# A sixth place for layer 1's split weight units, and one query buffer fewer

## The chip, the core and the metric

The kernel runs on one core of one Trainium2 chip. The metric is device time in microseconds (us) of one execution, and a kernel stands by the median of its runs. All texts below call the engines as the profile does: PE is TensorE (PEld its weight loads), DVE is VectorE, ACT is ScalarE, POOL is GpSimd, SP is SyncE, which here issues the DMAs.

## What is computed

The reference is a two-layer transformer block over 512 latent tokens and 256 context tokens of width 1024, in float32. Layer 0 is a mixer of windowed and dense grouped-query attention, layer 1 is differential attention over 8 heads, and a SwiGLU feed-forward follows each of them. The change lies in layer 1's attention. Cut to that, the reference is:

```python
def _odd_mixer(hx, hc, w_in, w_out, qn, kn, ...):
    q, k, v = jnp.split(h @ w_in, [qs, 2 * qs], axis=-1)   # w_in: 1024 x 3072
    q = _rope(_rms(q.reshape(b, n, 8, 2, 64), qn), cos, sin)
    k = _rope(_rms(k.reshape(b, n, 8, 2, 64), kn), cos, sin)
    # per head: two softmaxes a = 0, 1 over context and latent keys
    s = jnp.einsum('bqhad,bkhad->bhaqk', qb, k) * scale
    p = jax.nn.softmax(s, axis=-1)
    a = p[:, :, 0] - lam * p[:, :, 1]
    o = jnp.einsum('bhqk,bkhe->bqhe', a, v)                # then RMS norm, @ w_out
```

Only the latent tokens have queries in layer 1, so a latent tile of 128 tokens is projected to 384 columns of a head (q, k, v) and a context tile to 256 (k, v).

## The kernel before

**Split products.** Each large product is done as three matmuls on values split into a high and a low part: the high part is a copy of the value in the matmul's float type, made on ACT, and the low part is value minus high part, made by a subtraction on DVE or POOL. `project` (line 460) does `hi*hi`, `hi*lo` and `lo*hi` for each of the 8 slices of 128 input features, 24 matmuls for a tile of 128 tokens.

**Weight units.** The weights of one head are four units, each of 256 input features by 384 columns. `weight1` (line 649) asks `unit` (line 361) for one: three DMAs of 128 KB into a raw tile (line 365; the raw tiles are a ring of two, shared with other loads), a copy on ACT into the high part `wih` (line 370) and a subtraction on POOL into the low part `wil` (line 371). The raw tile is free when the subtraction has read it. The high and the low parts stand in pools of their own, `whi` and `wlo`, each a ring of `WBUF` = 5 places. A unit can be split when a place is free, that is when the last matmul of an earlier unit has read it. The units of heads 0 to 7 are numbered 0 to 31 below, unit u of head h being 4h + u; the four of head 0 are split earlier, during the feed-forward of layer 0.

**Order of the work.** PE's order is written out by hand (`manual_schedule`). Head 0 is projected first, unit by unit for its latent tiles. From then on the projection of head h + 1 is threaded through the attention of earlier tiles in half tiles: `halves` (line 1579) gives 12 steps for a head, one for the first four feature slices of a token tile (units 0 and 1, 12 matmuls) and one for the other four (units 2 and 3). Three steps go with each of the 32 pairs of head and query tile (`scores`, `transposed`, `values`). All tiles of a head use all four units, so units 0 and 1 are read for the last time in the head's last step but one, and units 2 and 3 in its last step.

After a tile's second half, `Proj1.finish` (line 672) copies the sums out of PSUM (`qkv`, line 677, ACT), does the norm and the rotation (ACT, DVE, POOL), and splits the query into `qd` (a copy on ACT at line 685 and a subtraction on DVE at line 686) and the key into `kd` (line 688 on ACT, line 689 on POOL). PE transposes both into `qpt` and `kpt` (lines 696 and 702) at least five steps after the tile's own, in `turned`. `qd` has three buffers.

The order on ACT, DVE, POOL and SP is not written by hand: a planner lays each engine's queue out ahead of time, by program order as priority and by its own estimates of when operands and places are ready. An engine then works its queue strictly in that order, so one that arrives at an instruction early stands still.

**Pools.** Pools are stretches of SBUF, stacked from two sides. `mix1` (`at`, line 1569) holds the attention's `qt`, `e`, `PT` and `o1`; `mw1` (`wp`, line 1564) holds `qkv`, `qz`, `qy`, `qd` and `kd`. A later pool that lies over an earlier one waits tile by tile for what was there.

Of the kernel before, what the change touches and what calls it, by code (L numbers as in the profile page):

```python
# [12 lines left out]
F32R = mybir.dt.float32r  # L13
# [6 lines left out]
P = 128  # L20
# [7 lines left out]
HD = 64  # L28
# [23 lines left out]
def bc(ap, pos, n):  # L52

    dims = [list(d) for d in ap.ap]
    return AP(ap.tensor, ap.offset, dims[:pos] + [[0, n]] + dims[pos:])
# [8 lines left out]
def backbone(es: ExitStack, tc: tile.TileContext, x, c, ctx, c_ctx, mod_w, mod_b, norm_mix_w, norm_ffn_w,  # L64
# [3 lines left out]
    nc = tc.nc  # L68
# [24 lines left out]
    def acc_tile(name, n=512, one=None):  # L93

        if one is None:
            one = turn["acc"] = 1 - turn["acc"]
        return p_1.tile([P, 512], F32, name=name, tag=f"acc{one}")[:, :n]
# [4 lines left out]
    def tr_tile(name, shape, dt=F32, one=None):  # L102
        if one is None:
            one = turn["tr"] = 1 - turn["tr"]
        return p_1.tile(shape, dt, name=name, tag=f"tr{one}")

    @contextmanager
    def behind(*names):

        with ExitStack() as st:  # L110
            for name in names:
                if name in turn:
                    st.enter_context(tc.issue_after(turn[name].ins))
            yield

    def f32(ap):
        return ap.bitcast(F32)
# [243 lines left out]
    def unit(pool, views, shape, bufs, name, sub=None, new_tile=raw_tile):  # L361

        raw = new_tile(shape, name + "r")
        for dst, src in views(raw):
            turn["load"] = nc.sync.dma_start(dst, src)
        p_hi, p_lo = pool if isinstance(pool, tuple) else (pool, pool)
        hi = p_hi.tile(shape, F32R, name=name + "h", tag="whi", bufs=bufs)
        lo = p_lo.tile(shape, F32R, name=name + "l", tag="wlo", bufs=bufs)
        with behind("pool_scale"):
            nc.scalar.copy(hi, raw)  # L370
            (sub or nc.vector).tensor_sub(lo, raw, f32(hi))
        return hi, lo
# [44 lines left out]
    def rotate_all(raw, h0, n, t, wc, tb, pool):  # L417

        sq = pool.tile([P, n * HD], F32, name="sq", tag="qz", bufs=2)
        nc.scalar.activation(sq, raw, AF.Square)  # L420
        ss = small.tile([P, n], F32, name="qss", tag="qss")
        nc.vector.tensor_reduce(ss, sq.rearrange("p (h d) -> p h d", d=HD), AX.X, ALU.add)
        r = rsqrt(ss, n, 1.0 / HD, "q")
        y = pool.tile([P, n, HD], F32, name="qy", tag="qy", bufs=2)
        rh = raw.rearrange("p (h d) -> p h d", d=HD)
        if t >= NTX:
            nc.vector.tensor_tensor(y, rh, wc[:, h0:h0 + n], ALU.mult)
            return y, r
        z = pool.tile([P, n, HD], F32, name="qz", tag="qz", bufs=2)
        nc.vector.tensor_tensor(z.rearrange("p h (a b) -> p (h a) b", b=2),  # L430
                                swap_pairs(raw), tb[:, t, 1].rearrange("p h (a b) -> p (h a) b", b=2), ALU.mult)
        nc.vector.tensor_tensor(y, rh, tb[:, t, 0], ALU.mult)
        nc.vector.tensor_add(y, y, z)
        return y, r
# [214 lines left out]
    def weight1(h, u, wh, sub, new_tile=raw_tile):  # L649

        def views(raw):
            for j in range(3):
                yield raw[:, :, j * P:(j + 1) * P], od_w_in[
                    0, u * 256:(u + 1) * 256, j * D + h * P:j * D + (h + 1) * P].rearrange("(j p) n -> p j n", p=P)
        return unit(wh, views, [P, 2, 384], WBUF, "wi", sub, new_tile)

    class Proj1:
# [14 lines left out]
        def finish(self, t, ps):  # L672

            n, wp, kT, qs = self.width(t), self.wp.pool, self.kT, self.qs
            m, h0 = (n - P) // HD, 0 if t < NTX else 2
            raw = wp.tile([P, 384], F32, name="qkv", tag="qkv", bufs=4)
            nc.scalar.copy(raw[:, :n], ps[:, :n])  # L677
            nc.gpsimd.tensor_copy(self.vv[:, t, :], raw[:, n - P:n])
            y, r = rotate_all(raw[:, :n - P], h0, m, t, self.wc, self.tb, wp)
            nc.gpsimd.tensor_tensor(y, y, bc(r, 2, HD), ALU.mult)  # L680
            nq = m - 2
            if nq:
                qd = wp.tile([P, 2, 2, 2, HD], F32R, name="qd", tag="qd", bufs=3)
                yb = bc(y[:, 0:2], 2, 2)
                nc.scalar.copy(qd[:, 0], yb)
                nc.vector.tensor_sub(qd[:, 1], yb, f32(qd[:, 0]))
            kd = wp.tile([P, 2, 2, HD], F32R, name="kd", tag="kd", bufs=3)
            nc.scalar.copy(kd[:, :, 0, :], y[:, nq:nq + 2])
            nc.gpsimd.tensor_sub(kd[:, :, 1, :], y[:, nq:nq + 2], f32(kd[:, :, 0, :]))

            def transposes():
                if nq:
                    pt = tr_tile("qpt", [P, 2, 2, P], F32R)
                    for j in range(2):
                        for a in range(2):
                            nc.tensor.transpose(pt[:, j, a, :], qd[:, j, a].rearrange("p a d -> p (a d)"), identr)
                    qt = self.qp.tile([P, 2, 2, P], F32R, name="qt", tag="qt", bufs=5)
                    nc.scalar.copy(qt, f32(pt))
                    qs[t] = qt
                pk = tr_tile("kpt", [P, 2, P], F32R)  # L700
                for a in range(2):
                    nc.tensor.transpose(pk[:, a, :], kd[:, a].rearrange("p a d -> p (a d)"), identr)
                nc.scalar.copy(kT[:, :, t * P:(t + 1) * P], f32(pk))
            return transposes
# [344 lines left out]
    def way_out1(xs, hidr, pool, places_w, places_h):  # L1049
# [7 lines left out]
        def ready_hid(f):  # L1057
            def views(raw):
                yield raw, ffn_w_out[1, f * P:(f + 1) * P, :]
            if f < len(places_w):  # L1060
                raw = raw_tile([P, D], "wdr")
                turn["load"] = nc.sync.dma_start(raw, ffn_w_out[1, f * P:(f + 1) * P, :])
                w, h = places_w[f], places_h[f]
                split_into(w, raw.rearrange("p (k c) -> p k c", k=4))
                split_into(h, hidr[f].rearrange("p (k c) -> p k c", k=2))
            else:
                w = [z.rearrange("p (k c) -> p k c", k=4) for z in unit(pool, views, [P, D], 5, "wd")]
                h = [pool.tile([P, 2, SEQ // 2], F32R, name=name, tag=name, bufs=5) for name in ("hdh", "hdl")]
                split_into(h, hidr[f].rearrange("p (k c) -> p k c", k=2))
            ready[f] = h, w  # L1070
# [86 lines left out]
    wp = Pool("mw0", "right")  # L1157
# [5 lines left out]
    for t in CTX_FIRST:  # L1163
        h = start.pool.tile([P, D], F32, name="nh", tag="nh", bufs=2)
# [56 lines left out]
    at = Pool("mix0")  # L1221
# [68 lines left out]
    if True:  # L1290
        for i, (b, t) in enumerate(steps):
# [38 lines left out]
            if t == 0:  # L1330
# [13 lines left out]
                wp = Pool("w0", "right")  # L1344
# [219 lines left out]
    wp = Pool("mw1", "right")  # L1564
    wh = (whi.pool, wlo.pool)
# [3 lines left out]
    at = Pool("mix1")  # L1569
# [5 lines left out]
    def new_head(ws):  # L1575
        h = len(state)
        state.append(Proj1(h, ws, tabs, wp, states[(7 - h) % 3].pool, at.pool))

    def halves():
        for h in range(1, 8):  # L1580
            new_head([weight1(h, u, wh, nc.gpsimd) for u in range(4)])
            for t in CTX_FIRST:
                ps = acc_tile("inps", one=0)
                state[h].sums(t, ps, range(4))
                yield t
                state[h].sums(t, ps, range(4, KT))
                late.append((count + 5, state[h].finish(t, ps)))
                yield t

    todo = halves()  # L1590

    def step():
# [16 lines left out]
    if True:  # L1609
# [117 lines left out]
        wp = Pool("w1", "right")  # L1727
# [203 lines left out]
```

## Time and profile before

| what | value |
|---|---|
| median of 3 runs | 1697.68 us |
| runs | 1694.51, 1697.68, 1697.99 us |
| span of the profiled execution | 1695.6 us |
| granted TensorE clock, mean | 0.992 |
| PE busy | 1631.5 us (96%) |
| DVE, ACT, POOL busy | 1146.7, 937.0, 696.4 us |

No device time is given for the profiled execution beside its span, so the span stands for it; it is 2.1 us under the median run and lies between the fastest and the other two. Busy time is a sum over the whole program, in which different stages have different limits; the stage that the change touches is roughly 955 to 1265 us of the span.

### The profile page before, as it was taken

How to read it: one execution, taken by the hardware profiler on the slowest of the kernel's cores; microseconds unless marked ns; L12 is line 12 of the kernel's file. 1: busy time of each engine (PE TensorE's matmuls, PEld its weight loads, DVE VectorE, ACT ScalarE, POOL GpSimd, SP SyncE). 2: the span in 40 equal slices, each digit the busy share in tenths (PEclk: the TensorE clock that was granted, in tenths of full speed). 3: DMA queues.
4: the chain of work that ended last, by engine and by line, in shares of the span. 5: the costliest groups of instructions: out<-in, count | busy, mean ns of one | idle time of the engine just before them, and what ended most of it. 6: DMA issues, size and time to landing. Idle time of an engine off the chain costs nothing. (4 is left out here: it accounts for less than half of the span.)

```text
span 1695.6 us, 28585 instructions
## 1 busy us (share of the span) xinstructions
PE 1631.5 (96%) x10390; PEld 1468.6 (87%) x10390; DVE 1146.7 (68%) x2014; ACT 937.0 (55%) x2011; POOL 696.4 (41%) x867
## 2 busy tenths in 40 slices
PE   6999999899999999999999989999999999999998
PEld 3977787677999999998777889999988899999887
DVE  3765656754799887767767656666666598887434
ACT  5565555745456665545554456666666555555320
POOL 2665554321346554412413366666664242221000
PEclk8999999999999999999999999999999999999999
DMA  9222221411455555439966311111112433331431
GB/s 319 69 71 74 70 70 50 164 60 38 129 167 172 164 159 162 134 108 347 296 184 189 99 43 38 48 42 44 50 45 97 125 93 102 111 101 57 137 99 62
DMA packets 218108, 194.64 MB, mean 115 GB/s; under 512 B 20016, under 2 KB 202864, under 8 KB 217968
## 3 DMA queue, kind: packets, MB, share of 16 engines
q1 hardware_dynamic: 217616, 192.62, 36.8%
q8 instruction: 81, 1.33, 0.3%
q14 instruction: 59, 0.48, 0.1%
q10 hardware_dynamic: 352, 0.21, 0.0%
HBM read 179.92 MB, written 12.87 MB: 114 GB/s over the span
## 5 line engine op out<-in xcount | busy, mean ns | idle before, releaser
L901 ACT CAST wbh<-wr 128x512 fp32r<-128x512 f32 x170 | 104.9, 621 | 130.2 <-PE p L933 73.4
L933 PE MATMUL p<-hT,wbh 128*128 128x256 f32 (+1 forms) x752 | 154.5, 299 | 0.0
L465 PE MATMUL inps<-wih,hT 128*128 128x384 f32 x512 | 144.2, 344 | 7.3 <-ACT qkv L677 7.3
L911 POOL TENSOR_TENSOR wbl<-wr,wbh 128x512 fp32r<-128x512 f32 x43 | 60.0, 1396 | 173.6 <-ACT wbh L901 173.6
L933 PEld LDWEIGHTS p<-hT,wbh 128*128 128x128 f32 x752 | 121.9, 191 | 0.2
L911 DVE TENSOR_TENSOR wbl<-wr,wbh 128x512 fp32r<-128x512 f32 x127 | 107.7, 858 | 21.0 <-ACT wbh L901 16.8
L933 PE MATMUL p<-hT,wbl 128*128 128x256 f32 (+1 forms) x376 | 111.9, 298 | 0.0
L933 PE MATMUL p<-t,wbh 128*128 128x384 f32 (+1 forms) x480 | 111.3, 318 | 0.0
L604 POOL TENSOR_SCALAR Pt<-Pt,rc 128x256 f32<-128x256 f32 (+3 forms) x96 | 74.6, 788 | 89.3 <-DVE rc L601 83.1
L231 POOL TENSOR_TENSOR modp<-modp 128x512 f32<-128x512 f32 x40 | 57.4, 1436 | 114.3 <-ACT modp L230 114.3
L465 PEld LDWEIGHTS inps<-wih,hT 128*128 128x128 f32 x512 | 93.3, 188 | 10.6 <-ACT qkv L677 9.7
L933 PE MATMUL p<-hTt,wbh 128*128 128x256 f32 (+1 forms) x480 | 101.0, 302 | 0.0
L887 POOL TENSOR_TENSOR wr<-wr 128x512 f32<-128x512 f32 x40 | 61.6, 1540 | 89.8 <-DVE ws L892 85.8
L933 PE MATMUL p<-b,wbh 128*128 128x384 f32 x368 | 93.8, 336 | 0.2 <-DVE c L961 0.2
L901 ACT CAST wbh<-ws 128x512 fp32r<-128x512 f32 x120 | 69.4, 579 | 43.1 <-PE p L933 29.0
L224 DVE SCALAR_TENSOR_TENSOR ma<-modw,cols,ma 128x256 f32<-128x256 f32 x140 | 89.2, 637 | 2.3
L592 ACT ACTIVATE Pt<-sc,nm 128x256 f32<-128x256 f32 (+3 forms) x96 | 67.6, 707 | 35.3 <-DVE nm L588 16.9
L465 PE MATMUL inps<-wil,hT 128*128 128x384 f32 x256 | 86.0, 336 | 0.0
L933 PEld LDWEIGHTS p<-t,wbh 128*128 128x128 f32 x480 | 82.9, 189 | 0.0
L911 DVE TENSOR_TENSOR wbl<-ws,wbh 128x512 fp32r<-128x512 f32 x120 | 81.7, 681 | 1.7 <-ACT wbh L901 1.6
L933 PEld LDWEIGHTS p<-hTt,wbh 128*128 128x128 f32 x480 | 78.3, 191 | 3.1 <-ACT modp L230 1.6
L230 ACT ACTIVATE modp<-modw,cols 128x256 f32<-128x256 f32 x160 | 68.4, 500 | 18.0 <-POOL ma L236 10.1
(355 smaller groups left out, 5217.9 us busy)
## 6 DMA issues: line engine op xcount, KB each, us to landing
modw<-in_mod_w_dram SPq DMA_DIRECT2D x96, 512.0 KB, 5.2
wr<-in_ffn_w_in_dram SPq DMA_DIRECT2D x176, 256.0 KB, 2.9
wdr<-in_ffn_w_out_dram SPq DMA_DIRECT2D x66, 512.0 KB, 3.7
wir<-in_od_w_in_dram SPq DMA_DIRECT2D x96, 128.0 KB, 2.3
hidm<-hid SPq DMA_DIRECT2D x44, 192.0 KB, 1.9
hr<-hidm SPq DMA_DIRECT2D x22, 192.0 KB, 3.5
x<-in_x_dram SPq DMA_DIRECT2D x8, 512.0 KB, 3.5
wir<-in_ev_w_in_dram SPq DMA_DIRECT2D x16, 256.0 KB, 3.5
```

The costliest lines, as they stand in the source:

```text
L224: nc.vector.scalar_tensor_tensor(acc, w[:, k], scale[k], acc, ALU.mult, ALU.add)
L230: nc.scalar.activation(pr[:, k], w[:, k], AF.Copy, scale=scale[k])
L231: nc.gpsimd.tensor_add(pr[:, 0:2], pr[:, 0:2], pr[:, 2:4])
L465: nc.tensor.matmul(ps, hs[j][:, k, :], ws[k // 2][z][:, k % 2, c0:c1], start=(k, j, z) == (0, 0, 0), stop=(k, j, z) == (KT - 1, 1, 0))
L592: turn["exp"] = nc.scalar.activation(p[:, :n], s, AF.Exp, bias=nm[:, c1], accum_out=sm[:, c1])
L604: nc.gpsimd.tensor_scalar(p[:, :n], p[:, :n], rc[:, hh:hh + 1], 1.0, ALU.mult, ALU.mult)
L887: nc.gpsimd.tensor_sub(w, raw[f, "G1"], w)
L901: nc.scalar.copy(hi, w)
L911: (nc.gpsimd if name == "G2" else nc.vector).tensor_sub(lo, raw[need[n]], f32(hi))
L933: nc.tensor.matmul(ps, w[:, k, :], H[b][h][:, k, :], start=first and k == 0 and q == 0, stop=final and k == 3 and q == 2, skip_group_check ...
```

## The change

The units whose number leaves 5 when divided by 6 (5, 11, 17, 23 and 29: head 1 unit 1, head 2 unit 3, head 4 unit 1, head 5 unit 3, head 7 unit 1) get their high and low parts in the attention's pool `at`, in a single place there; all others stay in the ring of five. `at` so grows by 6 KB per partition (two tiles of 2 x 384 float32). `qd` has two buffers in the place of three, by which `mw1` shrinks by 2 KB per partition. No instruction of arithmetic, no DMA and nothing in PE's order is added or removed.

```diff
@@ unit @@
         p_hi, p_lo = pool if isinstance(pool, tuple) else (pool, pool)
+        if isinstance(pool, tuple) and p_hi is p_lo:
+            bufs = 1
         hi = p_hi.tile(shape, F32R, name=name + "h", tag="whi", bufs=bufs)
         lo = p_lo.tile(shape, F32R, name=name + "l", tag="wlo", bufs=bufs)
@@ Proj1.finish @@
-                qd = wp.tile([P, 2, 2, 2, HD], F32R, name="qd", tag="qd", bufs=3)
+                qd = wp.tile([P, 2, 2, 2, HD], F32R, name="qd", tag="qd", bufs=2)
@@ halves @@
-            new_head([weight1(h, u, wh, nc.gpsimd) for u in range(4)])
+            new_head([weight1(h, u, (at.pool, at.pool) if (4 * h + u) % 6 == 5 else wh, nc.gpsimd) for u in range(4)])
```

## Prediction

> **What bounds the kernel now.** I read the page's busy times first, then the stage of the change by windows, then who waited for whom in it, then single moments of the timeline.
>
> ```profile
> span 1695.6 us, 28585 instructions
> PE 1631.5 (96%) x10390; PEld 1468.6 (87%) x10390; DVE 1146.7 (68%) x2014; ACT 937.0 (55%) x2011; POOL 696.4 (41%) x867
> ```
>
> ```profile
> 963.00:1000.00 37.00, 31.36 (x206) 29.39 (x204) 22.62 (x40) 21.73 (x55) 31.53 (x46) 1.00 0.24 67
> 1000.00:1264.00 264.00, 256.23 (x1794) 246.36 (x1793) 167.72 (x342) 170.69 (x443) 175.66 (x281) 1.00 0.15 42
> 984.00:1001.00 17.00, 14.07 (x104) 13.10 (x103) 9.03 (x19) 9.12 (x25) 15.00 (x27) 1.00 0.17 48
> ```
>
> The windows give length, then busy time of PE, PEld, DVE, ACT and POOL. In the steady part of layer 1's attention (1000 to 1264) PE is busy 256.2 of 264.0 us: all that anything could win there is 7.8 us. In the start of the stage (963 to 1000) PE is idle 5.6 of 37.0 us and POOL is the fullest engine but PE, and from 984 to 1001 POOL is busy 15.0 of 17.0 us, more than PE. So the reader has two stages: one bound by PE, with small holes, and a short one before it where POOL sets the pace.
>
> The chain of waits between 946 and 1300 us says who makes the holes (total us, times, longest):
>
> ```profile
> PEld inps L465 <- ACT qkv L677: 11.0, 11, 1.7
> ACT wih L370 <- PE inps L465: 4.8, 12, 0.6
> PEld inps L465 <- POOL wil L371: 2.6, 6, 1.2
> PE inps L465 <- POOL wil L371: 1.0, 1, 1.0
> ```
>
> PE waits longest for `qkv`, the copy out of its one PSUM bank of sums, which no place for weights touches. It waits for weights six times, 2.6 us in all. The 1.0 of the last row is the PE side of one of these six, so it is not added. The second row is the ring itself: twelve times the copy of a unit stood on ACT until PE had read the old one for the last time.
>
> One head border in the timeline (start, duration, idle before):
>
> ```profile
> 1017.00 0.84 ACT L370 CAST wih<-wir 128x768 fp32r<-128x768 f32 x1 [0.59 <-PE inps L465]
> 1018.04 0.83 ACT L370 CAST wih<-wir 128x768 fp32r<-128x768 f32 x1 [0.20 <-PE inps L465]
> 1023.43 0.84 ACT L370 CAST wih<-wir 128x768 fp32r<-128x768 f32 x1
> 1025.62 0.83 ACT L370 CAST wih<-wir 128x768 fp32r<-128x768 f32 x1
> ```
>
> ```profile
> 1017.91 2.05 POOL L371 TENSOR_TENSOR wil<-wir,wih 128x768 fp32r<-128x768 f32 x1 [1.97 <-ACT wih L370]
> 1020.32 1.84 POOL L371 TENSOR_TENSOR wil<-wir,wih 128x768 fp32r<-128x768 f32 x1
> 1024.98 1.84 POOL L371 TENSOR_TENSOR wil<-wir,wih 128x768 fp32r<-128x768 f32 x1
> 1027.86 1.82 POOL L371 TENSOR_TENSOR wil<-wir,wih 128x768 fp32r<-128x768 f32 x1
> ```
>
> ```profile
> 1026.88 0.19 PEld L465 LDWEIGHTS inps<-wil,hTc 128*128 128x128 f32 x1 [0.29 <-POOL wil L371]
> 1147.59 0.19 PEld L465 LDWEIGHTS inps<-wil,hTc 128*128 128x128 f32 x1 [1.20 <-POOL wil L371]
> ```
>
> These are units 1, 2 and 3 of head 2 and then unit 0 of head 3. The ring of five lets only unit 0 of a head be split a head early. Units 1 and 2 have long been loaded and wait in the two raw tiles for PE; unit 3 cannot even be loaded before unit 1's subtraction has freed a raw tile (1019.96), and its subtraction ends at 1026.82 while PE wants it at 1026.59. That is the 0.29. The same 0.3 comes at each border of heads 2 to 7, and once, at 1147.59, 1.20 because the load came late.
>
> **The change, part by part.**
>
> *The sixth place in the steady part.* With six places unit n takes over that of unit n − 6: units 0 and 1 of a head now take those of units 2 and 3 of the head before last, and can be split a head early; units 2 and 3 take those of the last head's units 0 and 1. At the border of head 2, PE frees these in the very step for whose matmuls the casts of 1017.00 and 1018.04 stand now. So units 2 and 3 get the two slots of units 1 and 2, with subtractions that end at about 1019.96 and 1022.16, some 4 us before PE wants unit 3. The two later slots (1023.43 and 1025.62) go to units 0 and 1 of the next head, which nobody waits for. All 2.6 us of waits for `wil` go: six borders, 2.62 by their single values. What is late next at the same place is `PT` before the `av` matmuls, which is made by ACT and DVE right behind; it has some tenths of slack there, except where ACT is held by a load (below). Bounds: 2.6 us of gain, or nothing if each 0.3 is only handed on. I take 2.6, since PE runs solid from that point on.
>
> *The standing of ACT* (4.8 us, twelve times) stays: the casts move to other units, not to other moments. It is no gain.
>
> *The start of the stage.*
>
> ```profile
> 984.63 0.34 PE L465 MATMUL inps<-wih,hT 128*128 128x384 f32 x1
> 984.65 7.14 SPq L365 DMA_DIRECT2D wir<-in_od_w_in_dram  x6
> 988.55 1.82 POOL L371 TENSOR_TENSOR wil<-wir,wih 128x768 fp32r<-128x768 f32 x1
> 992.39 0.37 PE L702 MATMUL kpt<-identr,kd 128*128 128x128 f32 x2 [0.86 <-POOL kd L689]
> 995.89 0.36 PE L702 MATMUL kpt<-identr,kd 128*128 128x128 f32 x2 [0.79 <-POOL kd L689]
> 1001.86 0.29 POOL L678 COPY vv<-qkv 128x128 f32<-128x128 f32 x1 [1.24 <-ACT qkv L677]
> 1004.41 0.29 POOL L159 TENSOR_SCALAR rs_q<-qss 128x4 f32<-128x4 f32 x1 [2.25 <-DVE qss L422]
> ```
>
> Here the ring pays out something that the kernel does not want. Unit 9 (head 2, unit 1) is loaded at 984.65 (the first of those DMAs) and now waits for a place until 1017. With six places it takes that of unit 3, which PE reads last at 984.97 (first row), so its cast and its subtraction can come as soon as the load has landed, and the planner fills a hole with them.
>
> Unit 8's subtraction stands at 988.55 in the middle of the work that PE waits for; I expect unit 9's next, between 990 and 1000. Each 1.85 us that POOL gets more there arrives at `kd` and so at PE, which already waits for `kd` at 992.39 and 995.89. After 1001 POOL has holes of 1.24 and 2.25 us, and the subtraction would cost nothing. Bounds: nothing, or 1.85 + 0.84 us if the cast on ACT hurts as well. I take 1.5, nearer to the full subtraction, because unit 8's was put in the same stretch. Units 5 to 7 of head 1 keep their times: they were held by raw tiles and loads, as unit 5's cast here, not by places.
>
> ```profile
> 974.54 0.83 ACT L370 CAST wih<-wir 128x768 fp32r<-128x768 f32 x1 [2.49 <-DMA wir<-in_od_w_in_dram]
> L465 PE MATMUL inps<-wih,hTc x256: 276/279/385, 955.4 to 1233.6; 128*128 128x256 f32 x128
> ```
>
> *The DMAs.* The same 84 loads of units 4 to 31, on the same queue. Unit 11's is issued when unit 9's subtraction frees a raw tile, some 25 us early; nothing waits behind it on SP but the next units' loads. No cost.
>
> *Two buffers for `qd`.* A query's copy may now have to wait for the transposes of the query two before it. Two of the 32 pairs, the first and the tightest, which is near the end of head 7:
>
> ```profile
> 987.83 0.46 PE L696 MATMUL qpt<-identr,qd 128*128 128x128 f32 x4
> 993.82 0.41 ACT L685 CAST qd<-qy 128x256 fp32r<-128x256 f32 x1 [0.65 <-POOL qy L680]
> 1260.03 0.54 PE L696 MATMUL qpt<-identr,qd 128*128 128x128 f32 x4
> 1262.79 0.41 ACT L685 CAST qd<-qy 128x256 fp32r<-128x256 f32 x1 [1.03 <-POOL qy L680]
> ```
>
> The transposes end at 988.29 and 1260.57, the copies two queries on start at 993.82 and 1262.79: 5.5 and 2.2 us to spare, and no other pair has less than 5. No cost; without that cover, ACT would stand, and behind it `qkv`, for which PE waits.
>
> *The pools' addresses.* `at` grows by 6 KB and the states behind it move; what lay there belongs to layer 0's way out, whose matmuls end before layer 1's first projection (955.4, the row above), while unit 5 is written after 974.5. No cost.
>
> *The sum* against the profiled span: 1695.6 − 2.6 + 1.5 = 1694.5 us. That execution is 2.1 us under the median, so as a median I forecast 1697.68 − 1.1 = 1696.6 us. About 0.2% (3.4 us) is what a measurement of this kernel can tell from no change, so this counts as no change.
>
> **The rivals.**
>
> *The start gains too* (faster). ACT stands 3.60 us for a load, `qkv` comes late and PE loses 1.43 us:
>
> ```profile
> 981.31 0.83 ACT L370 CAST wih<-wir 128x768 fp32r<-128x768 f32 x1 [3.60 <-DMA wir<-in_od_w_in_dram]
> 983.66 0.44 PE L465 MATMUL inps<-wih,hT 128*128 128x384 f32 x1 [1.43 <-ACT qkv L677]
> 989.55 0.39 PE L465 MATMUL inps<-wih,hTc 128*128 128x256 f32 x1 [1.09 <-ACT qkv L677]
> ```
>
> If the planner, seeing places free earlier, lays these casts otherwise, 1.43 and 1.09 go and unit 9 costs nothing: 1697.68 − 2.6 − 2.5 = 1692.6 us. For it: ACT's queue is laid out anew. Against it: that load waits for a raw tile, of which there are still two.
>
> *ACT is held by loads* (slower). ACT's queue is in order, and a cast that stands for its load holds all behind it:
>
> ```profile
> 1106.36 0.83 ACT L370 CAST wih<-wir 128x768 fp32r<-128x768 f32 x1 [1.23 <-DMA wir<-in_od_w_in_dram]
> 1107.73 1.49 PE L744 MATMUL av<-vv,PT 128*128 128x128 f32 x11 [0.58 <-ACT PT L739]
> ```
>
> Here PE lost 0.58 us. The two late slots now both belong to units loaded just before, twelve casts in six heads. It decides from eight casts on: 1696.6 + 8 × 0.58 = 1701.2 us, and all twelve give 1703.6. Against it: it happened at two of the border slots now.
>
> *Nothing moves*: the 0.3 is only handed to `PT`, unit 9 falls after 1001: 1697.7 us.
>
> *POOL's subtraction holds DVE as well.* The trace has such a case:
>
> ```profile
> 1067.56 1.83 POOL L371 TENSOR_TENSOR wil<-wir,wih 128x768 fp32r<-128x768 f32 x1
> 1067.77 1.64 DVE L726 SCALAR_TENSOR_TENSOR rt<-sm,nlam,rc 128x1 f32<-128x1 f32 x1
> L726 DVE SCALAR_TENSOR_TENSOR rt<-sm,nlam,rc 128x1 f32<-128x1 f32 x32 | 11.9, 372 | 1.1
> ```
>
> An operation of 0.37 us on average took 1.64 and ended with POOL's subtraction. If unit 9's does that in the start, where DVE feeds POOL, its full 1.85 and another 1.27 us are lost: 1697.68 − 2.6 + 1.85 + 1.27 = 1698.2 us. [...]
>
> **How the numbers follow.** The forecast 0.48; the start gains 0.20; ACT held by loads 0.16; nothing moves 0.06; DVE held too 0.10. Faster by over 0.2% is the second alone, 0.20; slower is the third alone, 0.16; the rest, 0.64, is no change. The range goes from 1692.6, the gaining start, to 1701.2, where loads decide; this leaves out the far ends of both, about 0.2 together.
>
> **What the profile of the changed kernel would show.** Right: no PEld wait for `wil` after 1000; unit 9's subtraction on POOL before 1001; PE's idle time up in 984 to 1001 and down by 2.6 in 1000 to 1264; no ACT wait before `qd` on PE. Wrong: `wil` waits that stay, longer ones for `qkv` or `PT` at the borders, more DMA waits before line 370's casts, or a difference outside 955 to 1265 us, where I have costed nothing.

## The result and the profile after

The changed kernel is slower: median 1702.76 us of 8 runs (1700.19 to 1707.12) against 1697.18 us for the kernel before (8 runs, 1691.58 to 1697.99) on the same chip, a ratio of 1.0039 with a 95% interval of 1.0027 to 1.0052. The ratio is about 6.6 us of loss (the two medians lie 5.6 apart) where 1.1 us of gain was forecast, and the median is above the top of the range (1701.2). The profiled execution of the changed kernel took 1700.55 us. Lines behind 367 are numbered two higher in it: 372 is the unit's cast, 373 its subtraction, 467 the projection, 679 the copy `qkv`.

The page after, busy times, and the same two windows as before (length; busy time of PE, PEld, DVE, ACT and POOL with counts; granted clock; DMA share; GB/s):

```profile
span 1698.8 us, 28587 instructions
PE 1632.1 (96%) x10390; PEld 1469.5 (87%) x10390; DVE 1146.0 (67%) x2014; ACT 937.4 (55%) x2011; POOL 698.3 (41%) x867
```

```profile
963.00:1000.00 37.00, 30.38 (x174) 28.68 (x173) 19.42 (x36) 19.02 (x47) 30.65 (x41) 0.86 0.27 77
1000.00:1264.00 264.00, 254.15 (x1777) 244.56 (x1776) 168.54 (x340) 167.81 (x435) 170.24 (x274) 1.00 0.13 39
```

No engine has more to do. In the start of the stage PE gets through 174 instructions in the 37 us where it did 206, and its granted clock is 0.86 where it was 1.00. In the steady part PE is idle 2.1 us more (254.15 busy, before 256.23), not 2.6 less.

Spans of single executions are a poor measure here: layer 1's first projection starts between 950.5 and 955.7 us in the profiles below, though little before it differs. So the stage is measured in itself, from PE's rows: the start, from head 0's first projection matmul to head 2's; and the steady part, from there to the end of head 7's last.

| kernel | start, us | steady, us | time against before (95% interval) |
|---|---|---|---|
| before | 68.35 | 239.16 | 1 |
| after | 72.97 | 241.21 | 1.0039 (1.0027 to 1.0052) |
| e1_qd2 | 68.21 | 238.34 | 1.0002 (0.9990 to 1.0013) |
| e2_late_ring | 68.14 | 241.17 | 1.0015 (1.0003 to 1.0028) |
| e3_late_ring_order | 68.06 | 237.96 | 1.0001 (0.9992 to 1.0011) |
| e4_after_order | 72.75 | 236.92 | 1.0015 (1.0004 to 1.0025) |
| e5_after_unit8 | 68.76 | 240.84 | 1.0012 (1.0001 to 1.0022) |
| e6_before_order | 68.33 | 246.43 | 1.0037 (1.0023 to 1.0052) |
| e7_late_mid | 68.09 | 243.71 | 1.0021 (1.0011 to 1.0031) |
| e8_late_mid_one | 69.67 | 236.78 | 0.9981 (0.9970 to 0.9992) |
| e9_after_mid | 67.02 | 236.47 | 0.9985 (0.9976 to 0.9994) |
| e10_five_mid | 68.19 | 243.48 | 1.0027 (1.0016 to 1.0038) |

The ratio of e4 leaves out one slow run of 3204.12 us.

After against before, the start is 4.6 us longer and the steady part 2.05 us: together 6.7 us, which is the loss that the ratio gives. The profiles and the runs agree less well elsewhere, by up to some 2 us (e8 is 1.1 us shorter in the stage and 3.2 us by its ratio), so a difference of about 1 us between two single profiles is weak evidence.

**The start.** ACT in the changed kernel (start, duration, idle before and what ended it):

```profile
978.25 0.83 ACT L372 CAST wih<-wir 128x768 fp32r<-128x768 f32 x1 [2.04 <-DMA wir<-in_od_w_in_dram]
978.99 0.36 ACT L705 CAST kT<-kpt 128x256 fp32r<-128x256 f32 x1
981.17 0.83 ACT L372 CAST wih<-wir 128x768 fp32r<-128x768 f32 x1 [1.82 <-DMA wir<-in_od_w_in_dram]
981.91 0.47 ACT L679 COPY qkv<-inps 128x384 f32<-128x384 f32 x1
...
982.74 0.46 ACT L679 COPY qkv<-inps 128x384 f32<-128x384 f32 x1
```

The cast of 981.17 is unit 8's (head 2, unit 0). In a ring of five its place is that of unit 3, read last at 984.97 in the profile before, and the cast came at 986.45, behind the two `qkv` copies. In a ring of six its place is unit 2's, free at 977.69, so it stands ahead of these copies. ACT idles 1.82 us for its load, and PE, which waits for the second of the copies (it ends at 983.20), stands 3.28 us where it stood 1.43:

```profile
979.63 0.34 PE L467 MATMUL inps<-wih,hT 128*128 128x384 f32 x1
983.25 0.69 PE L467 MATMUL inps<-wih,hT 128*128 128x384 f32 x1 [3.28 <-ACT qkv L679]
```

During that stand the granted clock falls to 0.50. Windows of the changed kernel, columns as above:

```profile
979.07:982.48 3.41, 0.90 (x6) 0.58 (x4) 0.06 (x1) 1.55 (x5) 2.50 (x3) 1.00 0.35 103
982.48:989.31 6.83, 6.06 (x26) 5.96 (x27) 4.96 (x10) 2.94 (x7) 5.47 (x9) 0.50 0.41 116
```

For 6.83 us PE runs at half the clock: the first matmul behind the stand takes 0.69 us (983.25) where the kernel before took 0.44 for it (983.66). The clock falls a second time at 996.15, for 3.41 us. The whole start, before first and then after, tells what each part costs:

```profile
955.38:1023.73 68.35, 60.64 (x402) 57.25 (x401) 39.27 (x80) 40.71 (x100) 46.02 (x70) 1.00 0.22 63
953.11:1026.09 72.98, 64.35 (x403) 61.19 (x401) 37.94 (x80) 41.27 (x101) 48.78 (x71) 0.93 0.22 65
```

For the same matmuls PE is busy 3.7 us longer and idle only 0.9 us longer (8.63 against 7.71): the longer stand of 1.85 us is in part made up by shorter waits behind it, and four fifths of the 4.6 us are slower matmuls.

Unit 9's subtraction came where the prediction put it, and `kd` and PE wait behind it (one wait of 1.90 where before had 0.86 and 0.79, so 0.25 us more):

```profile
989.22 1.83 POOL L373 TENSOR_TENSOR wil<-wir,wih 128x768 fp32r<-128x768 f32 x1
994.85 0.36 PE L704 MATMUL kpt<-identr,kd 128*128 128x128 f32 x2 [1.90 <-POOL kd L691]
```

**The steady part.** Waits of PEld there, the kernel before first (1023 to 1264), then the changed one (1026 to 1264); total us, times, longest:

```profile
PEld inps L465 <- ACT qkv L677: 5.6, 6, 1.6
PEld inps L465 <- POOL wil L371: 2.6, 6, 1.2
PEld av L744 <- ACT PT L739: 1.3, 2, 0.8
```

```profile
PEld inps L467 <- ACT qkv L679: 9.0, 11, 1.6
PEld av L746 <- ACT PT L741: 2.8, 3, 1.2
```

The waits for `wil` are gone, all 2.6 us. In their place stand five new ones for `qkv` (3.4 us) and longer ones for `PT`. The five are of one kind. ACT at the fourth query tile of the attention, before and then after, and PE after:

```profile
1032.71 0.90 ACT L720 ACTIVATE e<-sc,mx 128x768 f32<-128x768 f32 x1
...
1033.83 0.37 ACT L677 COPY qkv<-inps 128x256 f32<-128x256 f32 x1
1034.43 0.30 ACT L688 CAST kd<-qy 128x128 fp32r<-128x128 f32 x1 [0.23 <-POOL qy L680]
1034.64 0.90 ACT L720 ACTIVATE e<-sc,mx 128x768 f32<-128x768 f32 x1
```

```profile
1034.91 0.90 ACT L722 ACTIVATE e<-sc,mx 128x768 f32<-128x768 f32 x1
...
1035.80 0.89 ACT L722 ACTIVATE e<-sc,mx 128x768 f32<-128x768 f32 x1
...
1036.68 0.37 ACT L679 COPY qkv<-inps 128x256 f32<-128x256 f32 x1
```

```profile
1037.10 0.44 PE L467 MATMUL inps<-wih,hT 128*128 128x384 f32 x1 [0.61 <-ACT qkv L679]
```

Before, the copy that frees PE's bank of sums stood between the two exponentials; after, it stands behind both, and PE waits. With the sixth place the planner laid ACT's queue differently; e1 below, which changes `qd` alone, keeps the old order.

### The profile page after: what moved, and what is told of

It reads as the page before. It is cut to its first block, busy times and chain, and to the rows that moved or that the text cites. A ratio compares the mean times of both kernels' runs of the same rounds, so it can differ in the third digit from the quotient of the medians.

```text
span 1698.8 us, 28587 instructions
## 1 busy us (share of the span) xinstructions
PE 1632.1 (96%) x10390; PEld 1469.5 (87%) x10390; DVE 1146.0 (67%) x2014; ACT 937.4 (55%) x2011; POOL 698.3 (41%) x867
## 3 DMA queue, kind: packets, MB, share of 16 engines
q8 instruction: 81, 1.33, 0.3%
```

## The experiments

The sums of a head are counted by token tile: tiles 0 to 3 (first to fourth) are latent, 4 and 5 (fifth and sixth) are context.

**e1: the query's two buffers alone.**

```diff
-  qd = wp.tile(..., tag="qd", bufs=3)
+  qd = wp.tile(..., tag="qd", bufs=2)
```

> The kernel before with two buffers for qd in the place of three, and no sixth place. Theory (planner's queues): the loss of 6.6 us comes from the order of ACT's queue, which this edit leaves as it is on every engine, so no change, within 2 us of before. Rival (fewer buffers or moved addresses): a part of the 6.6 us is here already, 2 us or more slower, with ACT standing before line 685.

Measured: 1.0002, start 68.21, steady 238.34 us; every engine's order is that of the kernel before. This half of the change costs nothing that the runs can tell. In the changed kernel the tightest pair is again near the end of head 7:

```profile
1264.44 0.54 PE L698 MATMUL qpt<-identr,qd 128*128 128x128 f32 x4
1267.19 0.41 ACT L687 CAST qd<-qy 128x256 fp32r<-128x256 f32 x1 [1.01 <-POOL qy L682]
```

The transposes end at 1264.98, 2.2 us ahead of the copy. The 0.8 us by which its steady part differs from before's, with the same order, is what single profiles of this stage vary by.

**e2: the sixth place from head 2 on (unit 11 the first in it).**

```diff
+  (at.pool, at.pool) if h > 1 and (4 * h + u) % 6 == 5 else wh
```

> The changed kernel, but the first unit with a place in the attention's pool is 11 and not 5, so that the start has the ring of five as before and only heads 3 to 7 have the sixth place. Theory: the start costs 4.6 of the 6.6 us, because a place that is free early lets unit 8's cast be queued on ACT ahead of the copies of head 0's sums, PE stands 3.3 us for them and its clock drops to half; that goes here, and what is left is the steady part, about 2 us slower than before, with a repeated wait of PE for qkv of 0.7 to 0.85 us in the middle of heads 4 to 7. Rival (the steady part or the addresses cost it): still 5 us or more slower.

Measured: 1.0015, as the theory had it; start 68.14 us (as before), steady 241.17 us (as after). The two losses are separate: the start's belongs to the places that come free for heads 1 and 2.

**e3 and e4: ACT's old order, held by hand,** with the late sixth place (e3) and with the change in full (e4). The edit, without the lines that name the copy and move the start of the exponential behind it:

```diff
+  if a and state.h * NTX + t in held_exps:     # fourth query tile, heads 0 to 5
+      yield
+  with behind(*(("qkv",) if a and state.h * NTX + t in held_exps else ())):
       turn["exp"] = nc.scalar.activation(e, s, AF.Exp, ...)
```

> As the kernel with the sixth place from unit 11 on, and at the fourth query tile of heads 0 to 5 the second exp is queued on ACT behind the copy of the sums (line 677 of before), as the kernel before had it; every other queue but DVE's stays. Theory: the repeated wait of 0.7 to 0.85 us for qkv goes, the 0.3 us for wil stays gone, so 1 to 3 us faster than before. Rival (the repeated wait has another cause, such as POOL being late): the waits for qkv stay, about 2 us slower than before.

> The changed kernel in full, with the second exp of the fourth query tile of heads 0 to 5 queued on ACT behind the copy of the sums, as the kernel before had it. Theory: the steady part gains its 2.6 us in the place of losing 2, so the total is some 2 us slower than before (4.6 lost in the start); PE's clock falls to half near 983 us again. Rival (the start is a chance of one execution): about 2 us faster than before, and no half clock near 983.

Measured: the steady part falls from 241.17 to 237.96 us in e3 and from 241.21 to 236.92 us in e4, and the waits for `qkv` in the steady part are six again. The row of e4 (1020 to 1265):

```profile
PEld inps L467 <- ACT qkv L679: 5.1, 6, 1.6
```

So the swapped order costs 3.2 to 4.3 us, more than the whole gain from the `wil` waits. With it held, e4's steady part is 2.24 us shorter than before's, close to the 2.6 that the prediction took. In time e4 stays at 1.0015, since its start is still 72.75 us, with a granted clock of 0.87 from 963 to 1000 (0.86 in the changed kernel) and 0.69 us again for the first matmul behind a stand of 3.18 us (984.38); the rival, a chance of one execution, is out. e3 stays at 1.0001 and so misses the 1 to 3 us of gain that were expected: its stage is shorter by 1.5 us in the profile, which the runs don't show.

**e5: unit 8 behind the copies,** the rest of the change as it is:

```diff
+  with behind(*(("qkv03",) if (h, u) == (2, 0) else ())):   # copy of latent tile 3 of head 0
       return unit(wh, views, ...)
```

> The changed kernel in full, with one edit: unit 8's split (head 2, unit 0) is queued on ACT behind the copy of head 0's fourth sum, so that it no longer stands ahead of the copies of the second and third; unit 9 stays as early as in the changed kernel. Theory (the cast that waits for its load ahead of two copies is what the start lost): the start falls from 72.97 us to about 68.35 + 1.5 = 69.9, PE's stand of 3.28 us before 983.25 goes, and the granted clock stays at 1.00 there; with the steady part as in the changed kernel the time is 1.0018 to 1.0025 of the kernel before. Rival (unit 9's subtraction on POOL at 989.22 is the price, as the prediction had it): the start stays at 72 to 73 us and the time at about 1.004.

Measured: start 68.76 us, steady 240.84, time 1.0012 (1.0018 to 1.0025 was expected). Window of the whole start, and PE rows of it:

```profile
951.92:1020.68 68.76, 60.16 (x402) 57.22 (x401) 38.14 (x80) 41.34 (x101) 48.50 (x71) 1.00 0.24 69
```

```profile
979.61 0.44 PE L467 MATMUL inps<-wih,hT 128*128 128x384 f32 x1 [0.85 <-ACT qkv L680]
986.71 0.39 PE L467 MATMUL inps<-wih,hTc 128*128 128x256 f32 x1 [2.28 <-ACT qkv L680]
990.22 0.37 PE L705 MATMUL kpt<-identr,kd 128*128 128x128 f32 x2 [1.55 <-POOL kd L692]
```

One cast's place in ACT's queue is worth 4.2 us, with a clock of 1.00 again. PE's idle time hardly changes: 8.60 us here, 8.63 in the changed kernel. What goes is 4.2 us of busy time, so the cast costs by the falls of the clock, which followed stands of 3.28 and 1.90 us there and follow none of 0.85, 2.28 and 1.55 us here. Unit 9, early as in the changed kernel, leaves 0.4 us: the last two waits (and 0.64 at a later `kd`) are 1.7 us more than before's 1.09, 0.86 and 0.79; 0.58 comes back at the first (before 1.43), and the rest in small waits and in PE's busy time (60.16 us, before 60.64). The rival, unit 9's subtraction as the price, is out.

**e6: the swapped order in the kernel before,** with five places:

```diff
+  with behind(*(("exp",) if t == 5 and self.h > 1 else ())):
       nc.scalar.copy(raw[:, :n], ps[:, :n])                 # qkv
```

> The kernel before with five places, and one edit: from head 2 on, the copy of the sixth sum stands on ACT behind the second exponential of the fourth query tile, as it does in the changed kernel. Theory (the order on ACT alone makes the new waits for qkv): PE stands six times some 0.7 to 0.85 us for that copy, the steady part goes from 239.16 to 242.5 to 244, the waits for wil of 2.6 us stay, and the time is 1.002 to 1.003 of the kernel before. Rival (the order costs only together with the earlier units): the steady part stays within 1 us of 239.16 and the time within 0.1%.

Measured: 1.0037, steady 246.43 us. Waits there (1021 to 1268):

```profile
PEld inps L465 <- ACT qkv L678: 13.8, 12, 1.7
PEld inps L465 <- POOL wil L371: 2.6, 6, 1.2
```

The order alone makes six new waits and costs 7.3 us in the stage. That is more than the theory said: each new wait is about 1.4 us, not 0.7 to 0.85. The kind is shown; what sets its size was not tried.

**e7 and e8: the casts off the border.** What e3 still loses are `PT` waits where ACT stands for a load. Both kernels are e3 with the splits of units 0 and 1 queued in the middle of the head before; in e7 behind its first and second sum's copies, in e8 both behind the first's.

```diff
+  with behind(*((f"qkv{h - 1}{u}",) if h > 2 and u < 2 else ())):     # e7; in e8 f"qkv{h - 1}0"
       return unit(wh, views, ...)
```

> The kernel with the late sixth place and the old order on ACT (68.06 us of start, 237.96 us of steady part), and one edit: from head 3 on, the splits of units 0 and 1 are queued on ACT behind the copies of the first and second sum of the head before, and so off the head's border. Theory (what is left at the borders is ACT that stands for loads, 2.8 us of PT waits): these waits go, the steady part falls to 235 to 237 us, and the time is 0.998 to 0.9995 of the kernel before. Rival (a cast in the middle of a head delays the exponentials and copies there by as much): the steady part is 238 to 241 us and the time 1.000 to 1.002.

> As the run before it, but both units are queued behind the copy of the first sum of the head before. If the place of the casts matters little, as long as it is off the border, the steady part is within 0.7 us of the other's; if two casts in a row (1.7 us) hold up the exponentials there, it is 1 to 4 us longer than the other's.

Measured: e7 is slower than before, 1.0021, and its steady part of 243.71 us lies above both ranges given for it; e8 is faster, 0.9981, and its steady part is 6.9 us shorter than e7's, which neither expectation had. Steady waits of e7, then of e8:

```profile
PEld inps L467 <- ACT qkv L680: 13.1, 11, 1.7
PEld av L752 <- ACT PT L747: 0.5, 1, 0.5
```

```profile
PEld inps L467 <- ACT qkv L680: 6.4, 6, 1.6
PEld av L752 <- ACT PT L747: 0.5, 1, 0.5
```

Both clear the `PT` waits but one. In e7 `qkv` waits come back twice a head, because copies of later sums now stand behind `qd`, `kd` or both exponentials; 6.7 us of waits lie between the two kernels, and 0.0040 in time, 6.8 us. Two casts in a row, which might have held up the exponentials, are the better place. e8's start is 1.6 us longer than e3's, though up to its end every engine's order is e3's, so the moved casts are not the cause. POOL stands 2.80 us there for a small load, `subln`, which in e3 took 2.09:

```profile
979.78 0.56 POOL L1651 TENSOR_SCALAR subln<-subln 128x128 f32<-128x128 f32 x1 [2.80 <-DMA subln<-in_od_subln_dram]
980.43 2.14 POOL L373 TENSOR_TENSOR wil<-wir,wih 128x768 fp32r<-128x768 f32 x1
```

Whether that explains all of the 1.6 was not tried.

**e9: the change in full with ACT's order held** as in e8, from head 2 on (so units 8 and 9 too). **e10: five places with unit 0 moved** the same way.

```diff
+  with behind(*((f"qkv{h - 1}0",) if h > 1 and u < 2 else ())):       # e9
+  with behind(*((f"qkv{h - 1}0",) if h > 2 and u < 1 else ())):       # e10
```

> The changed kernel in full (sixth place from unit 5 on), with the order on ACT held in two ways: the second exponential of the fourth query tile stands behind the copy of the sixth sum, and the splits of units 0 and 1 of heads 2 to 7 stand behind the copy of the first sum of the head before. Theory (what the change loses is only ACT's order): start 68 to 69.5 us at a clock of 1.00, steady part 236 to 237.5 us, time 0.997 to 0.999 of the kernel before. Rival (with the place free from unit 5 on, the start is laid worse whatever is done with units 8 and 9): start above 70.5 us and time 0.999 to 1.001.

> The kernel before with five places, and one edit: from head 3 on, the split of unit 0, the only one that a ring of five lets be split a head early, stands on ACT behind the copy of the first sum of the head before. Theory (the sixth place is needed for the gain): unit 3's split stays last before PE's need, the waits for wil of 2.6 us stay, only the PT waits (1.3 us) go, steady part 238 to 239.2 us, time 0.999 to 1.000. Rival (the casts' place off the border is all, the sixth place does nothing): the waits for wil go as well, steady part below 237.2 us, time about 0.998.

Measured: e9 0.9985, start 67.02 us, steady 236.47 us; the steady part and the time lie in what the theory gave, the start a little below it. e10 1.0027, steady 243.48 us. Start window and steady waits of e9, then the steady waits of e10:

```profile
963.00:1000.00 37.00, 32.93 (x217) 31.22 (x217) 23.23 (x41) 22.94 (x56) 31.48 (x44) 1.00 0.20 56
```

```profile
PEld inps L467 <- ACT qkv L680: 6.4, 6, 1.6
PEld av L752 <- ACT PT L747: 0.5, 1, 0.5
```

```profile
PEld inps L465 <- ACT qkv L678: 10.6, 11, 1.6
PEld inps L465 <- POOL wil L371: 2.4, 6, 0.8
```

With the same sixth place and the same two query buffers, the change is 0.15% faster instead of 0.39% slower. e10 missed both expectations: the `wil` waits stay, so this move doesn't clear them with five places, but the move drew five more `qkv` waits as in e7, which hides what the place of the casts alone is worth. e8 and e9 are the versions that beat both kernels; their intervals overlap. The gain is not the sixth place's alone: e3, with the same place and the exponential held but the casts at the border, stood at 1.0001 where e8 has 0.9981.

## Why the prediction was wrong

**The start (taken at +1.5 us, measured +4.6).** The step that failed is the list of what comes earlier. It took up unit 9 alone and quoted unit 8's old place only as a pattern. Every unit gets a place one unit sooner, and unit 8's came free at 977.69 in the place of 984.97, in time to stand ahead of the copies that PE waits for. Unit 9 was predicted rightly in place (989.22); in e5 it cost 1.0 us with what came with it, and 0.58 came back, which is the first rival in small: the earlier places do help `qkv` at that point. The clock's fall was in no step. It is most of the loss: e5 has the idle time of the changed kernel to 0.03 us, no fall, and a start that is 4.2 us shorter.

**"Units 5 to 7 of head 1 keep their times".** Nearly so, as the wait for loads before their casts stayed (2.04 us at 978.25). But the sentence asked only about units that were held by loads, not about the next one, which was held by its place.

**The steady part (taken at −2.6 us, measured +2.05).** The `wil` term was right: no such wait is left, and units 2 and 3 come early, with subtractions that end at 1022.30 and 1024.51:

```profile
1020.25 2.05 POOL L373 TENSOR_TENSOR wil<-wir,wih 128x768 fp32r<-128x768 f32 x1 [1.96 <-ACT wih L372]
1022.66 1.85 POOL L373 TENSOR_TENSOR wil<-wir,wih 128x768 fp32r<-128x768 f32 x1
```

What failed is "I take 2.6, since PE runs solid from that point on", and behind it "the casts move to other units, not to other moments". ACT's slots were taken as fixed. They are an outcome of the same planning that the change moved, and five times `qkv` fell behind an exponential. e2 with e3, and e4 with the changed kernel, put 3.2 to 4.3 us on that; for the changed kernel, 2.24 us of gain with the order held less 4.29 us for the order is the 2.05 measured.

**"ACT is held by loads"** (chance 0.16) had the sign, the outcome and part of the mechanism; that 1702.76 lies between its 1701.2 and 1703.6 is luck. Its price was to come from eight to twelve border casts; in the steady part of the profile only a few such stands reach PE, 1.3 to 1.5 us of `PT` waits more than before. Where it decided was the start, one cast and 1.82 us, because PE was already waiting for what stood behind it. **"POOL's subtraction holds DVE as well"** found no victim in unit 9's subtraction (989.22 to 991.05): DVE had nothing ready beside it.

```profile
991.74 0.29 DVE L424 TENSOR_REDUCE qss<-sq 128x2 f32<-128x128 f32 x1 [3.91 <-ACT sq L422]
```

Long operations of DVE beside a subtraction are there: beside unit 8's (from 982.08, 1.81 us) one took 1.75 us from 982.42, where the next of its line, at 985.18, took 0.41; in the kernel before one took 1.59 us beside that unit's (989.07), where one of its line took 0.41 at 1066.60. No run tried what lengthens them; that POOL holds DVE was the author's reading of such pairs.

**The standing of ACT for PE** (4.8 us, twelve times) stayed to the tenth, as said:

```profile
ACT wih L372 <- PE inps L467: 4.8, 12, 0.6
```

**The two buffers of `qd`, the DMAs, the addresses** at nothing: e1 bears out the first, and with the order held e9 leaves no loss for the others.

The last part of the prediction named "longer ones for `qkv` or `PT` at the borders" as what would make it wrong; that is what showed, the `qkv` ones some 11 us behind the border (1037.10, with head 2's first matmul at 1026.09). It gave that no chance of its own, though it noted that ACT's queue is laid out anew and used it only as a possible gain.

## What to carry to other kernels

When a planner lays the queues, a freed place is not a local edit: ask for each operation that may come earlier, not only the one that waited longest, what it would be queued ahead of, and whether its own operand will have landed by then. Here the dear mistakes were a cast that waits for its load, and a long exponential, queued on ACT ahead of the short copy that PE waits for. Hold that copy's order first and then add the buffer: the kernel with it was 0.39% slower without such an order and 0.15% faster with it.

## What the runs showed of the hardware

A stand of PE cost more than its length here: e5 and the changed kernel have nearly the same idle time in the start (8.60 and 8.63 us), and 4.2 us lie between them. The clock fell to 0.50 some 2.5 us into the stand of 3.28 us and stayed there 6.83 us, and it fell again at 996.15 for 3.41 us. In the 3.41 us before the two falls PE was busy 0.90 us (above) and 1.51 us:

```profile
992.74:996.15 3.41, 1.51 (x13) 1.37 (x13) 1.35 (x4) 1.46 (x4) 3.25 (x7) 1.00 0.31 85
```

The stands of 2.28 us in e5 and 2.44 us in e8 left the clock at 1.00. The second fills much of this stretch, with PE busy 1.57 us in it:

```profile
985.68:989.09 3.41, 1.57 (x13) 1.58 (x14) 1.79 (x2) 1.85 (x6) 3.40 (x4) 1.00 0.00 0
```

Between 45 and 1690 us the traces of the kernel before and of the changed kernel show three falls to 0.50 each, five of 3.41 us and the one of 6.83. In the 3.41 us ahead of each fall, at 1.00, PE was busy 0.96, 1.75 and 1.44 us in the kernel before (falls at 197.83, 849.78 and 1269.62) and 1.33, 0.90 and 1.51 us in the changed one (197.43, 982.48 and 996.15). PE had worked for a quarter to a half of each of these stretches, and the stretch of e8, with 1.57 us, lies within what they span and left the clock at 1.00. What decides is not settled by these runs.
